# A hybrid decoder layer in one kernel: another queue for token loads, and another order of hand-over for token tiles, partial results, weight sums and counts

## The chip, the core and the metric

The kernel runs on one core of a Trainium2 chip. A core has four compute engines that each take their instructions in order: TensorE for matrix products (with a queue of its own for loading weights into the array), VectorE, ScalarE, and GpSimd. A fifth, SyncE, here only issues DMA transfers; GpSimd and ScalarE issue some too. All transfers are carried out by 16 DMA engines. The metric is the device time of one execution in microseconds (us), the median of several runs.

## What is computed

The reference is one decoder layer with two groups of heads side by side, for 1024 prompt tokens and 8 single decode tokens (1032 tokens in all, each 2048 wide), in float32:

```python
def project(h, w_in, b_i, b_f):          # h = rmsnorm(x): 1032 tokens x 2048
    (aq, ak, av, iq, ik, iw, az, mq, mk, mv, mi, mf, mo, mz) = jnp.split(h @ w_in, split_points, axis=-1)
...
def dsa_prompt(q, k, v, qi, ki, wi):     # sparse attention: the index picks 256 of the earlier tokens
    scores = indexer_scores(qib, ki, wib)          # relu(qi . ki) weighted by wi, summed over 16 heads
    _, idx = lax.top_k(scores, topk)
    return sparse_attend(qb, gather_rows(k, idx), gather_rows(v, idx), valid)
...
def mlstm_run(q, k, v, ig, lf, C0, n0, m0, chunk):   # a recurrent memory, four heads of 128 x 256
...
def merge(x, att_o, p, h_ml, ml_norm_w, w_out):
    a = att_o * jax.nn.silu(p['az'])
    mo = rmsnorm(h_ml) * jax.nn.sigmoid(p['mo']) * jax.nn.silu(p['mz'])
    return x + jnp.concatenate([a, mo], axis=-1) @ w_out
```

The decode tokens do the same against a paged cache of 4096 past tokens each: their index scores over the past are reduced to the best 256 rows, which are gathered from the cache. The outputs are the normalized results of both groups of tokens, the keys and values, and the memory's states.

## The kernel before

**Precision.** A float32 operand of a matrix product is split in two: `H`, the value rounded to the matrix unit's format, and `L`, what is left. A product is the sum of three: H by H, L by H, H by L. So every weight tile and every token tile is cast by ScalarE (`H`) and subtracted by VectorE (`L`) before TensorE uses it. The rows of the profile show such pairs as `wH`, `wL` (weights) and `xH`, `xL` (tokens).

**Stages of TensorE's main work.** A clock of the plan, the *step*, counts tiles of 128 columns of `w_in`; each step is one tile, in four quarters.

1. *Steps 0 to 20, plain projection* (`proj`, matmuls at L1544, 344 or 388 tokens wide). Steps 1 to 8 make the queries of the index, whose results `evac` takes out of the matrix unit's banks and writes as `iqe` (L379). Steps 9 to 20 make the keys `ki` of the index, and the attention's keys, values and queries.
2. *Steps 21 to 60, the gate stage* (`gate_stage`, matmuls at L1727, 258 tokens wide). Forty tiles are taken as twenty 2 x 2 block problems, and each of these is done by Strassen's scheme with seven products instead of eight: 140 products of 48 matmuls. A product has a *kind* from 1 to 7, which says which sum or block of weights, and which sum or block of tokens, it multiplies. The order is: kinds 4 and 6 in pairs (products 0 to 39), all of kind 1 (40 to 59), all of kind 3 (60 to 79), all of kind 2 (80 to 99), kinds 5 and 7 in pairs (100 to 139). After each half of a product `tick` is called: a tick is 1/7 of a step, a product two ticks, so product n begins at step 21 + 2n/7.
3. The output projection (`quarter` and what follows it, matmuls at L2092), again by Strassen's scheme.

**Token tiles.** Strassen's scheme needs five sums and blocks of the tokens (each 2048/2 deep by 516 wide). `job_prep` makes them in steps of `(k, c)`: 16 steps, each loads a tile `X` (`load`, two transfers, L1402), scales it on VectorE (L1410), makes differences in a tile `O` (L1416 and L1417), and stores `O` (L1419) and part of `X` (L1420) to a scratch array `xsD`. It asks for `X` two steps ahead, from three buffers, and has one buffer for `O`. Loads and stores are both issued by GpSimd.
In the gate stage three *slots* of eight tile pairs hold what the products need; a slot is refilled by `fill(slot, op)`, which puts eight entries on a list. Each tick takes one entry off it: a load from `xsD` on SyncE (L1680), and three ticks later its cast and subtraction (L1674 and L1675). `None` on the list is a tick without a load.

**Partials.** Kinds 4 and 6 leave a sum per block that kind 1 adds to, then kind 3, and so on. Each partial is 258 KB: `put` stores it to `spD`, `get` loads it back into one of four buffers `ev` (L1746), and `combine` adds the new product out of the banks (L1822). In the phases of kinds 1, 3 and 2 `ask` is called for the first partial before the phase, and for that of product i + 1 halfway through product i.

**Weight sums.** Kinds 0 to 3 multiply sums of weight blocks. `job_usum` makes these in main memory with DMAs alone: `copy` writes one block to `usD` (L1432), `plus` adds another onto it with an accumulating DMA on GpSimd (L1436). The order is sums 0 and 1 together for all twenty problems, then sum 3 for all, then sum 2 for all. Copies of sums 0 and 3 go out on SyncE, the rest on GpSimd.

**The work beside.** The rest are *jobs*: generators whose `yield` hands back a number of units. Each `Job` has a first step, a last step and a weight (its units in all). Three *lanes* run one job each at a time; at each quarter or tick a lane goes on with its job until the units done are in line with the time left to its last step. A larger `yield` is thus a longer pause before the job's next instructions are put on the list. Lane 0: `gates`, `index` (`job_index`: scores of the prompt's index at L468 to L473, and the choice of its 256 tokens, whose masks `biasS` SyncE stores at L562), `att`, `ml`. Lane 1: `prep`, `dscore`, `dsel` (`job_dsel`: for the decode tokens, a search of the 256th best score bit by bit; each round counts on VectorE into `cb`, L1062, and sums the counts over partitions with a small matmul, L1064), `qrows`, `datt` (gathers at L1294), `dml`. Lane 2: `usum`. `wget`, which gives a product its weights, first runs lane 2 on if the sum isn't made yet.

**What sets the order.** The Python code lists the instructions; a scheduler then plays the list against the engines and fixes each engine's order, work under `tc.high_priority()` first. `pin` (`tc.keep_in_program_order`) holds an instruction behind the one listed just before it on the same engine. On the chip each engine and each queue then goes strictly in that order, waiting on semaphores.

## Time and profile before

| | |
|---|---|
| median of 3 runs | 1986.03 us (1983.48 to 1994.43) |
| the profiled execution | 1999.2 us |
| its span, first to last instruction | 1997.4 us |
| mean granted clock of TensorE | 0.983 |
| TensorE busy | 1910.9 us, 96% of the span, 13422 matmuls |
| VectorE, ScalarE, GpSimd busy | 1406.6, 918.6, 388.6 us |
| moved by DMA | 474.46 MB, 238 GB/s over the span |

How to read it: the span is one profiled execution; busy times leave out instructions that only issue transfers, so SyncE has none. "L1727" is a line of the kernel. In a group of instructions, what is written stands left of the arrow and what is read right of it, then the shapes, then the count, the busy time, the mean of one in ns, and the engine's idle time ahead of them with what ended most of it. "PEld" is TensorE's loading of weights; "SPq" and "POOL" with a DMA are the issuing of transfers by SyncE and GpSimd. "A <- B: x, n, m" in a view of waits says that A waited x us for B in n waits, the longest m us. The granted clock is 1 when TensorE runs at full rate; after an idle time it is lower for a while.

### The profile page before, as it was taken

The page shows a single profiled execution, that of the slowest core. Times are in us where ns is not written, and L with a number is a line of the kernel's source. Part 1 is how long each engine was busy: PE and PEld are TensorE (multiplying, and loading weights), DVE is VectorE, ACT ScalarE, POOL GpSimd, SP SyncE. Part 2 cuts the span into 40 slices and gives each one's busy share as a digit, 9 for nine tenths or more (in the row PEclk, how much of TensorE's full clock was granted, in tenths as well). Part 3 has the DMA queues.
Part 4 walks back from the last instruction along what each step waited for, and adds up shares of the span by engine and source line. Part 5 has one row for each costly group of instructions (what it writes and reads, how often), then busy time and mean ns, then how long its engine had stood idle before and what let it go on. Part 6 is the DMA issues. An engine that isn't in the chain of part 4 may idle for free. (4 is left out here: it accounts for less than half of the span.)

```text
span 1997.4 us, 37376 instructions
## 1 busy us (share of the span) xinstructions
PE 1910.9 (96%) x13422; PEld 1829.6 (92%) x13422; DVE 1406.6 (70%) x3341; ACT 918.6 (46%) x1826; POOL 388.6 (19%) x486
## 2 busy tenths in 40 slices
PE   9979999999979999889999999999999999999997
PEld 9979899999959999778999989999999999977876
DVE  8555658758798797483565656576888676777797
ACT  8112364464255652111455555445556334455645
POOL 0232112231110000232001111001112131107632
PEclk9989999999989999998999999999999999999999
DMA  7577666579865447996888999578998858898866
GB/s 258 168 206 221 192 203 186 167 205 245 271 167 168 157 159 235 353 344 213 255 217 224 291 297 241 153 246 258 293 318 306 226 190 273 276 323 291 286 198 220
DMA packets 252918, 474.46 MB, mean 238 GB/s; under 512 B 40549, under 2 KB 116133, under 8 KB 246333
## 3 DMA queue, kind: packets, MB, share of 16 engines
q1 hardware_dynamic: 217261, 356.70, 54.7%
q0 software_dynamic: 21504, 107.32, 20.6%
q10 hardware_dynamic: 13968, 8.06, 1.4%
q8 instruction: 105, 1.72, 0.4%
q14 instruction: 80, 0.66, 0.1%
HBM read 381.54 MB, written 174.32 MB: 278 GB/s over the span
## 5 line engine op out<-in xcount | busy, mean ns | idle before, releaser
L1727 PE MATMUL pj<-xH 128*128 128x258 f32 x1920 | 550.1, 288 | 21.5 <-DVE ev L1822 20.8
L1727 PE MATMUL pj<-xH,xL 128*128 128x258 f32 x1920 | 550.1, 287 | 1.7 <-issue 1.7
L1727 PE MATMUL pj<-xL,xH 128*128 128x258 f32 x1920 | 548.8, 286 | 0.8 <-issue 0.7
L1727 PEld LDWEIGHTS pj<-xH 128*128 128x128 f32 x1920 | 366.9, 191 | 26.2 <-DVE ev L1822 20.3
L1727 PEld LDWEIGHTS pj<-xH,xL 128*128 128x128 f32 x1920 | 367.7, 192 | 3.5 <-issue 2.5
L1727 PEld LDWEIGHTS pj<-xL,xH 128*128 128x128 f32 x1920 | 367.6, 191 | 2.1 <-issue 0.6
L1544 PE MATMUL pj<-xH,wH 128*128 128x344 f32 (+1 forms) x816 | 267.0, 330 | 12.2 <-DVE iqe L379 11.4
L1544 PE MATMUL pj<-xL,wH 128*128 128x344 f32 (+1 forms) x816 | 266.3, 327 | 0.0
L1544 PE MATMUL pj<-xH,wL 128*128 128x344 f32 (+1 forms) x816 | 266.3, 327 | 0.0
L1436 POOL DMA_DIRECT2D usD<-in_wa_dram x80 | 66.3, 927 | 615.8 <-DMA usD<-in_wa_dram 392.6
L256 ACT CAST wH<-wraw 128x512 fp32r<-128x512 f32 (+2 forms) x151 | 89.7, 608 | 177.8 <-PE pj L1544 83.6
L1544 PEld LDWEIGHTS pj<-xH,wH 128*128 128x128 f32 x816 | 154.7, 190 | 14.4 <-DVE iqe L379 12.3
L1544 PEld LDWEIGHTS pj<-xL,wH 128*128 128x128 f32 x816 | 154.8, 190 | 0.8 <-DVE xL L314 0.3
L1544 PEld LDWEIGHTS pj<-xH,wL 128*128 128x128 f32 x816 | 154.9, 190 | 0.2
L257 DVE TENSOR_TENSOR wL<-wraw,wH 128x512 fp32r<-128x512 f32 (+2 forms) x151 | 103.7, 700 | 54.9 <-ACT wH L256 53.1
L2092 PE MATMUL pj<-wH,sH 128*128 128x512 f32 x336 | 132.0, 393 | 1.2 <-ACT wH L2076 0.9
L2092 PE MATMUL pj<-wL,sH 128*128 128x512 f32 x336 | 126.3, 394 | 6.8 <-DVE wL L2081 6.8
L2092 PE MATMUL pj<-wH,sL 128*128 128x512 f32 x336 | 131.4, 392 | 0.0
L470 ACT ACTIVATE rl<-bank 128x512 f32<-128x512 f32 (+2 forms) x160 | 79.8, 522 | 77.9 <-DVE s L473 30.6
L473 DVE SCALAR_TENSOR_TENSOR s<-rl,wiN,s 128x512 f32<-128x512 f32 (+2 forms) x150 | 94.9, 655 | 21.5 <-ACT rl L470 19.3
L468 PE MATMUL bank<-ki,qi 128*128 128x512 f32 (+2 forms) x320 | 82.3, 378 | 10.0 <-ACT rl L470 4.1
L1710 ACT CAST xH<-wL 128x1024 fp32r<-128x1024 f32 x46 | 48.2, 1049 | 94.5 <-PE pj L1727 37.6
(485 smaller groups left out, 4415.3 us busy)
## 6 DMA issues: line engine op xcount, KB each, us to landing
usD<-in_wa_dram POOLq DMA_DIRECT2D x80, 512.0 KB
wraw<-in_wt_dram SPq DMA_DIRECT2D x144, 256.0 KB
usD<-in_wa_dram SPq DMA_DIRECT2D x40, 512.0 KB
usD<-usD POOLq DMA_DIRECT2D x40, 512.0 KB
wraw<-in_wa_dram SPq DMA_DIRECT2D x78, 256.0 KB
wraw<-in_wo_dram SPq DMA_DIRECT2D x64, 256.0 KB
ev<-spD SPq DMA_DIRECT2D x62, 258.0 KB
spD<-ev SPq DMA_DIRECT2D x60, 258.0 KB
```

The costliest lines, as they stand in the source:

```text
L256: a = SC.copy(H[:, s, :cols], raw[:, s, :cols])
L257: return a, V.tensor_tensor(L[:, s, :cols], raw[:, s, :cols], H[:, s, :cols].bitcast(F32), OP.subtract)
L468: PE.matmul(p[:, :cn], qi[:, h % 4, :], ki[x][:, c0:c0 + cn], start=(x == 0), stop=(x == 1))
L470: SC.activation(r[:, :cn], p[:, :cn], AF.Relu)
L473: v = V.scalar_tensor_tensor(s[:, c0:c0 + cn], r[:, :cn], wv, s[:, c0:c0 + cn], OP.mult, OP.add)
L1436: pin(G.dma_start(usD[n, i], src, accum_op=OP.add, max_dma_last_dim=8192))
L1544: m = PE.matmul(ps[:cols, :cn], w_[:, k, :cols], x_[kk][:, c0:c0 + cn], start=(kk == ends[0] and z == 0), stop=(kk == ends[1] and z == 2))
L1710: SC.copy(H, raw[2])
L1727: PE.matmul(ps[c], w_[:, q, ks], x[y][:, c * CS:c * CS + CS], start=(first and q == 0 and k == 0 and z == 0), stop=(q == 1 and k == 3 and ...
L2092: PE.matmul(ps[b], S_[x][:, b * 128:b * 128 + 128], T_[y], start=(k == 0 and z == 0), stop=(k == 7 and z == 2))
```

## The change

Five things are changed; the computation isn't.

1. `load` of `job_prep` issues the tokens' loads on SyncE instead of GpSimd (32 transfers). The job's last step goes from 11 to 12.
2. `fill` gets a parameter `gap`: after each load that many empty ticks stand on the list (1 by default, 3 for slot 0 ahead of kind 1, 2 for slot 0 ahead of kind 2). The refill of slot 2 for kind 2 moves from ahead of kind 1 to ahead of kind 3.
3. In the phases of kinds 1, 3 and 2 two partials are asked for ahead of the phase, and product i asks for that of product i + 2.
4. `job_usum` becomes two jobs in lane 2: `early sums` (sums 0 and 1, and sum 3 of the first eight problems; steps 9.6 to 28.5) and `late sums` (the rest; steps 33 to 47). Before, one job ran from step 12 to 46.
5. In `job_dsel` the count and its sum over partitions are two functions, `count` and `total`, with a `yield` between them in each round; its weight is 4000 units larger and its last step is 27.5 instead of 26 (`qrows` follows, 28 instead of 27). `index` gets a second `yield 3000` ahead of its first scores, begins at 9.4 instead of 9.6, and ends at step 25 instead of 26.5.

The core of the diff:

```diff
@@ job_index
             for n in range(3):
                 load_q(n)
             yield 3000
+            yield 3000
@@ job_dsel
-            def total(src, n=1):
+            def count(src, n=1):
                 with nc.allow_low_precision("counts"):
                     V.tensor_reduce(cb[:, :n * NB], src, AX.X, OP.add)
+
+            def total(n=1):
                 p = bank()
                 PE.matmul(p[:, :n * NB], onesb, cb[:, :n * NB], start=True, stop=True)
                 return p[:, :n * NB]
...
-                c = total(g3[:, :n].rearrange("p y b g -> p (y b) g"), n).rearrange("p (y b) -> p y b", y=n)
-                yield 1700 if n == 1 else 3400
+                count(g3[:, :n].rearrange("p y b g -> p (y b) g"), n)
+                yield 1200 if n == 1 else 2200
+                c = total(n).rearrange("p (y b) -> p y b", y=n)
+                yield 500 if n == 1 else 1200
@@ job_prep
-                    pin(G.dma_start(X[:, y], A["xT"][k + 8 * y].rearrange("p (h t) -> p h t", h=2)[:, :, c:c + CS]))
+                    pin(SY.dma_start(X[:, y], A["xT"][k + 8 * y].rearrange("p (h t) -> p h t", h=2)[:, :, c:c + CS]))
@@ job_usum
-        for i in range(NP + 1):
+        for i in range((NP + 1) * early):
...
-        for n, src in ((3, None), (2, 1)):
+        for n in (3, 2):
             for i in range(NP):
+                if early != (n == 3 and i < NE):
+                    continue
@@ lanes
-                   Job("index", T_AK + 0.6, 26.5, 3000 + sum(map(ix_weight, groups)), lambda: job_index(groups)),
+                   Job("index", T_AK + 0.4, 25.0, 6000 + sum(map(ix_weight, groups)), lambda: job_index(groups)),
...
-             Lane([Job("usum", T_AK + 3.0, 46.0, 8 * NP, job_usum)])]
+             Lane([Job("early sums", T_AK + 0.6, 28.5, 4 * NP + 2 * NE, lambda: job_usum(True)),
+                   Job("late sums", 33, 47.0, 4 * NP - 2 * NE, lambda: job_usum(False))])]
@@ gate_stage
-        def fill(slot, op):
+        def fill(slot, op, gap=1):
             for k in range(8):
                 fills.append((*slots[slot][k], xsD[op, k]))
+                fills.extend([None] * gap)
...
-        fill(0, 2)
-        fill(2, 1)
+        fill(0, 2, 3)
...
         ask(0, 0)
+        ask(0, 1)
         for i in range(NP):
             ps = two()
-            product(1, i, 1, ps, True, asker(0, i + 1))
+            product(1, i, 1, ps, True, asker(0, i + 2))
             with tc.high_priority():
                 put(1, i, combine(ps, got.pop(0), OP.add))
+        fill(2, 1)
         fill(1, 3)
```

The phases of kinds 3 and 2 get the same two lines for their partials, and the refill of slot 0 ahead of kind 2 a gap of 2.

More of the change, by code (lines that the diff above doesn't have):

```diff
@@ L1067, in job_dsel @@
             V.tensor_scalar(ge, sD, 0.0, None, OP.is_ge)
-            c = total(ge)
+            count(ge)
+            yield 2000
+            c = total()
             V.tensor_scalar(pos, c, float(TOPK), None, OP.is_ge)
@@ L1092, in job_dsel @@
             V.tensor_tensor(eq, sD, bc(tf), OP.is_equal)
-            c = total(ge)
+            count(ge)
+            yield 2000
+            c = total()
             V.tensor_scalar(rr, c, -1.0, float(TOPK), OP.mult, OP.add)
@@ L1423, in body, with job_usum @@
     sums = set()
-    def job_usum():
+    NE = 8
+    def job_usum(early):
         def parts(i):
@@ L1484, in body @@
     lanes = [Lane([Job("gates", 5, T_AK - 0.5, 12500, job_gates),
-                   Job("index", T_AK + 0.6, 26.5, 3000 + sum(map(ix_weight, groups)), lambda: job_index(groups)),
+                   Job("index", T_AK + 0.4, 25.0, 6000 + sum(map(ix_weight, groups)), lambda: job_index(groups)),
                    Job("att", T_G + 8, 44.5, 2 * 2 * sum(2 * (1 + (i + 1) * 0.5) for i in range(8)) + 18, job_att, att_free),
                    Job("ml", T_G + 20, 57.0, 39, job_ml, lo_done)]),
-             Lane([Job("prep", 3, T_AK + 2, 1 + 16 * 2, job_prep),
+             Lane([Job("prep", 3, T_AK + 3, 1 + 16 * 2, job_prep),
                    Job("dscore", T_AK + 3, 18.0, 24 + 128 + 2, job_dscore),
-                   Job("dsel", T_AK, 26.0, 2000 + 31 * 1700 + 10000 + 16 * 2800 + 2000, job_dsel),
-                   Job("qrows", T_G + 0.2, 27, 1, job_qrows),
+                   Job("dsel", T_AK, 27.5, 4000 + 31 * 1700 + 12000 + 16 * 2800 + 2000, job_dsel),
+                   Job("qrows", T_G + 0.2, 28, 1, job_qrows),
                    Job("datt", T_G + 7.5, 32.5, 10000 + 8 * 5000 + 34000 + 5 * 2500 + 8000 + 8000 + 5000, job_datt, ix_free),
                    Job("dml", T_G + 20, 55.0, 28000 + 16 * 2500 + 5000, job_dml, hi_done)]),
-             Lane([Job("usum", T_AK + 3.0, 46.0, 8 * NP, job_usum)])]
+             Lane([Job("early sums", T_AK + 0.6, 28.5, 4 * NP + 2 * NE, lambda: job_usum(True)),
+                   Job("late sums", 33, 47.0, 4 * NP - 2 * NE, lambda: job_usum(False))])]
     gateV = gateS.rearrange("(k p) r -> k p r", p=128)
@@ L1866, in gate_stage @@
         ask(0, 0)
+        ask(0, 1)
         for i in range(NP):
             ps = two()
-            product(1, i, 1, ps, True, asker(0, i + 1))
+            product(1, i, 1, ps, True, asker(0, i + 2))
             with tc.high_priority():
                 put(1, i, combine(ps, got.pop(0), OP.add))
+        fill(2, 1)
         fill(1, 3)
         ask(1, 0)
+        ask(1, 1)
         for i in range(NP):
             ps = two()
-            product(3, i, 0, ps, True, asker(1, i + 1))
+            product(3, i, 0, ps, True, asker(1, i + 2))
             with tc.high_priority():
@@ L1886, in flush @@
                 ready.extend((state["u"], k) for k in ks)
-        fill(0, 0)
+        fill(0, 0, 2)
         ask(2, 0)
+        ask(2, 1)
         for i in range(NP):
             ps = two()
-            product(2, i, 2, ps, True, asker(2, i + 1))
+            product(2, i, 2, ps, True, asker(2, i + 2))
             with tc.high_priority():
```

## The prediction

> **What bounds the kernel now.** I read the page's head first, then the time by stretches, then TensorE's waits, and only after that each engine and queue that ends one of those waits. The page:
>
> ```profile
> span 1997.4 us, 37376 instructions
> PE 1910.9 (96%) x13422; PEld 1829.6 (92%) x13422; DVE 1406.6 (70%) x3341; ACT 918.6 (46%) x1826; POOL 388.6 (19%) x486
> ```
>
> TensorE is the bound, so a change can only win back TensorE's idle time and the half clock that follows it. The stretches (length, then PE, PEld, DVE, ACT, POOL busy with instruction counts, granted clock, DMA share, GB/s) say where those lie:
>
> ```profile
> 75.00:100.00 25.00, 25.00 (x146) 24.95 (x145) 13.94 (x27) 4.45 (x8) 4.46 (x6) 1.00 0.85 256
> 100.00:150.00 50.00, 39.39 (x202) 38.73 (x201) 27.51 (x57) 9.57 (x17) 17.69 (x24) 0.90 0.71 207
> 200.00:225.00 25.00, 21.37 (x123) 20.86 (x122) 9.73 (x21) 5.68 (x12) 4.20 (x6) 0.93 0.95 254
> 225.00:525.00 300.00, 300.00 (x1977) 296.22 (x1976) 213.78 (x616) 146.98 (x320) 63.49 (x71) 1.00 0.69 196
> 550.00:600.00 50.00, 38.07 (x188) 30.19 (x189) 47.90 (x112) 28.55 (x52) 5.26 (x8) 0.90 0.61 162
> 600.00:775.00 175.00, 175.00 (x1450) 173.18 (x1449) 149.88 (x412) 95.55 (x151) 2.11 (x3) 1.00 0.54 166
> 800.00:950.00 150.00, 126.47 (x942) 119.41 (x941) 80.55 (x126) 25.03 (x34) 45.42 (x45) 0.92 0.92 302
> ```
>
> Four losses follow. In 100 to 150 TensorE issues 202 matmuls where the stretch before gives 146 in 25 us, so 292 in 50: 90 are missing, 90/146 x 25 = **15.4 us**. In 200 to 225, 3.6 us are idle and the clock is 0.07 short over 25 us, 1.8: **5.4 us**. In 550 to 600, 11.9 idle and 50 x 0.10 of clock: **16.9 us**. In 800 to 950, at the 1450/175 = 8.29 matmuls per us of 600 to 775, 1243 were due and 942 came: 301/8.29 = **36.3 us** (idle 23.5 and clock 150 x 0.08 = 12 give about the same). Who ends the waits (total, times, longest):
>
> ```profile
> PE pj L1727 <- DVE ev L1822: 20.8, 9, 5.0
> PE pj L1544 <- DVE iqe L379: 11.4, 3, 6.1
> PE bank L1064 <- DVE cb L1062: 6.5, 2, 4.8
> PE bank L468 <- DMA ki<-kS: 3.6, 2, 2.1
> ```
>
> One wait for each loss: evictions of index tiles (first), `ki` (second), the count for dsel (third), the adding of partials (fourth).
>
> **Token loads to SyncE.** VectorE's waits from 75 to 150, GpSimd's and SyncE's from 60 to 260, then GpSimd's queue:
>
> ```profile
> DVE X L1410 <- DMA X<-in_xT_dram: 15.4, 9, 2.3
> DVE O L1416 <- DMA xsD<-O: 14.7, 7, 5.2
> ```
> ```profile
> POOL X L1402 <- DMA xsD<-X: 76.4, 13, 7.3
> ```
> ```profile
> SPq L253 <- DVE wL L257: 35.1, 11, 8.6
> ```
> ```profile
> 109.36 1.45 POOL L1402 DMA_DIRECT2D X<-in_xT_dram  x2 [6.29 <-DMA xsD<-X]
> 110.81 0.77 POOL L1419 DMA_DIRECT2D xsD<-O  x1
> 111.58 0.73 POOL L1420 DMA_DIRECT2D xsD<-X  x1
> 119.61 1.45 POOL L1402 DMA_DIRECT2D X<-in_xT_dram  x2 [7.30 <-DMA xsD<-X]
> ```
>
> A step of prep is a ring: the load of X waits until the store of an earlier X has landed (6.3 us), takes 1.45 us to issue, and the two stores of the step stand behind it on GpSimd. That is one step in 119.6 - 109.4 = 10.2 us. VectorE, bound in order, waits for X and for O, and the eviction of the index tile stands behind those waits. With the loads on SyncE the stores no longer stand behind a waiting load, so O's store leaves earlier; the 15.4 us of waits for X should mostly go, the 14.7 for O partly. Prep also gets 9 steps of the plan instead of 8. All 32 loads now cost SyncE issue time, some 0.4 us each by its rows for tiles of this size further down (1.27 for three), 13 us over the 180 of prep, which its waits cover; behind each one that waits stand weight loads and index stores. The gain lies between 15.4 and, if SyncE's weights come late, a loss (a rival below). O's half is not clearly cured, so I take half, **7.7 us**.
> A rule of the Trainium skill ("DMA: Bandwidth & Descriptors", section "Issuing engines are not separate DMA queues") speaks against this: transfers issued from any engine run on the same 16 DMA engines, so another issuer saves only issue time. By it this term would be near nothing; the row that bears on it is the store standing behind the 6.29 us wait, which is order on a queue and not bandwidth.
>
> **Index, early sums and the ki wait.** The second `yield 3000` lets the plan put 6000 of 25,956 units per step, 0.231 steps, between loading `ki` and the first score, before it was 3000 of 23,782, 0.126. With some 27 us per step (12 tiles from about 201 to 526) that is 2.9 us more lead against 3.6 us of waiting. But sums now start at step 9.6 instead of 12 and prep runs to 12, at a DMA share of 0.95 already. I take **1 us**, between 0 and 5.4. The faster index (9% more units per step) adds at most 0.09 x 213.78 = 19 us of VectorE to 225 to 525, where it is busy 71% and TensorE never stops: nothing.
>
> **dsel's counts.** The whole kernel's row of this matmul:
>
> ```profile
> L1064 PE MATMUL bank<-cb,onesb 128*128 128x24 bf16 (+1 forms) x18 | 3.4, 186 | 6.7 <-DVE cb L1062 6.5
> ```
>
> The same instructions are issued; only the matmul is handed over 1200 or 2200 units (about 0.1 to 0.18 steps) after the count, so products stand before it. Its 6.5 us with their share of the clock, 5.0 x 6.5/11.9 = 2.7, make 9.2 us. But VectorE is busy 47.90 of 50 us there: a count that is late for that reason is late after a step too. Half of it, **5 us**; the ends are 0 and 16.9 (if index and dsel, planned apart now, empty the whole stretch).
>
> **Partials, token tiles, sums.** The product stage from 815 on. First VectorE's waits of 800 to 935 and two of its rows, then SyncE's queue and the count of product matmuls up to 815:
>
> ```profile
> DVE ev L1822 <- DMA ev<-spD: 11.3, 4, 4.8
> ```
> ```profile
> 838.03 0.76 DVE L1822 TENSOR_TENSOR ev<-pj,ev 128x258 f32<-128x258 f32 x2 [1.23 <-DMA ev<-spD]
> ```
> ```profile
> 897.87 0.76 DVE L1822 TENSOR_TENSOR ev<-pj,ev 128x258 f32<-128x258 f32 x2 [4.75 <-DMA ev<-spD]
> ```
> ```profile
> 521.14 1.27 SPq L1680 DMA_DIRECT2D xL<-xsD  x3
> ```
> ```profile
> 823.15 8.94 SPq L1680 DMA_DIRECT2D xL<-xsD  x8
> 832.41 0.32 SPq L1746 DMA_DIRECT2D ev<-spD  x1
> ```
> ```profile
> 526.00:815.00 289.00, 239.68 (x1920) 235.67 (x1920) 0.98 0.65 196
> ```
>
> 1920/48 = 40 products end at 815, so product 41's partial was asked at 832.4, behind a run of eight token tiles that held SyncE 8.9 us, and used at 838.0; TensorE stood 5.0 us. Asking two ahead puts that request in front of the phase and every later one a product, at least 48/8.29 = 5.8 us, earlier, against VectorE waits of at most 4.8. The ring has four buffers: asked two ahead, a buffer is taken again two products after its store was issued, 8 us or more, still longer than a store of this size took above (6.3 to 7.3). So the 11.3 us go, with their share of the clock, 12 x 11.3/23.5 = 5.8: **17.1 us**. The lower end is 0 (requests still late because the transfers are), the upper the whole 36.3.
> The spreading itself I cost at nothing, because in SyncE's rows it already doesn't hold: the first token tiles of the product stage go out at 521, before its first product, though the list puts twenty empty ticks ahead of them. They leave when their buffer is free, and the casts are what the gap moves. If that cover fails the gain is inside the 36.3.
> The sums: GpSimd and SyncE around the end of index.
>
> ```profile
> 643.84 0.52 POOL L1432 DMA_DIRECT2D usD<-usD  x1 [4.75 <-DMA usD<-in_wa_dram]
> 782.35 1.56 POOL L1436 DMA_DIRECT2D usD<-in_wa_dram  x2 [137.99 <-DMA usD<-in_wa_dram]
> ```
> ```profile
> 809.06 1.81 POOL L1294 DMA_INDIRECT ck<-in_ck_dram,idxs  x1 [0.31 <-PE bank L1727]
> ```
> ```profile
> 774.02 0.53 SPq L562 DMA_DIRECT2D biasS<-gt  x1
> 774.60 0.49 SPq L1432 DMA_DIRECT2D usD<-in_wa_dram  x1
> ```
>
> GpSimd stood 138 us for a copy that SyncE issued behind index's last store, then made up its sums in front of the gathers, so that both fell into 800 to 950. With the sums' first part planned to be over at 28.5 and index at 25.0, the copies should be out before that store, and the gathers start free. I count this as the cover for the partials' term and add nothing. The late sums end at step 47, the last is needed by the product at 49.3 (21 + 99 x 2/7), the first of them is made at 38.7 and needed at 43.9: no new wait.
>
> **Sum.** 7.7 + 1 + 5 + 17.1 = 30.8 us. The profiled execution took 1999.2 us, its span and 1.8 around it, so 1968.4; it lies 13 us above the median shown, and I carry the difference over: 1986.0 - 30.8 = **1955 us**.
>
> **Rivals.**
> *The queue doesn't matter* (also the skill's rule above): prep's ring is the landing of its stores, whoever issues the loads. For it: the 14.7 us for O; against it: the 15.4 for X. Without 7.7: 1963.
> *The partials come late anyway*, since transfers and not requests are slow: for it, share 0.92 and 302 GB/s over 150 us; against it, the run of eight in front of the request. Without 17.1: 1972.
> *Product 60 waits for its last token tile.* Its casts are now handed to ScalarE on ticks 83 to 111 instead of 83 to 90, each behind what att was given by then (2.69 units a tick, so 82 units, eight pairs, instead of 26). ScalarE, then product matmuls:
>
> ```profile
> 990.01 1.15 ACT L1674 CAST xH<-xL 128x516 fp32r<-128x516 f32 x2
> ```
> ```profile
> 1059.33 0.62 ACT L617 CAST qH<-qL 128x512 fp32r<-128x512 f32 x1 [0.51 <-PE bank L634]
> ```
> ```profile
> 983.00:1059.00 76.00, 44.36 (x310) 40.08 (x310) 1.00 0.67 188
> ```
>
> The last of these tiles was cast at 990, att's ninth pair was near 1059. If att starts no earlier than now, the 310 product matmuls between move back, 310/8.29 = 37 us. Against it: with gathers earlier, att starts earlier, and from some 70 us before product 60 on it costs nothing. 37 - 30.8: 1992.
> *SyncE becomes the queue that waits* (the slower side). The 76.4 us that GpSimd waits for landed stores move to SyncE between 75 and 255; its slack there is the 35.1 us for which weight loads wait for their buffer. The rest, 41.3, delays weights. It decides where a load of X is issued more than the weights' lead before its store lands, above all after step 9.6, where prep's stores now stand behind sums on GpSimd. 41.3 instead of a gain of 7.7, the others kept: 1986 + 41.3 - 23.1 = 2004. Against it: a store is issued about 10 us, a step, before the load that waits for it and lands in 6 to 7.
>
> **How the numbers follow.** Forecast 0.45 (by itself 1940 to 1972), queue 0.13, partials 0.17, product 60 0.13, SyncE 0.12. About 0.5%, 10 us, is what a measurement can tell from no change: faster is below 1976, slower above 1996. Faster: 0.45 + 0.13 + two thirds of 0.17 = 0.69. Slower: SyncE 0.12 and a quarter of product 60, 0.16 rounded up for mishaps; the rest 0.15. The range goes from 1935 (7.7 more from the first stretch and 12 from the other bounds) to 2003, just under the SyncE case.
>
> **What would show it.** Right: no idle of GpSimd for `xsD<-X`, over 240 matmuls in 100 to 150; no VectorE wait for `ev<-spD` after product 40, and over 1050 matmuls in the 150 us around it; GpSimd without a 138 us wait; `L1064` idle under 4 us. Wrong: SyncE waiting for `xsD<-X` with TensorE waiting for weights before 260; TensorE waiting on `xH L1674` near product 60; token tiles that do leave tick by tick, which would make my nothing for the spreading false.

## The result

The changed kernel takes 2010.95 us (median of 4, 2007.50 to 2013.76), the kernel before 1984.76 us on the same chip: 1.0123 of before, 95% interval 1.0083 to 1.0163, so about 24 us slower. The forecast was 1955 us, the range 1935 to 2003.

Single executions of one kernel scatter by several us: in one comparison 25 of before lay between 1979 and 2003 us. So the ratios below, with their 95% intervals, rest on 4 to 12 executions of a kernel beside before on the same chip. They are estimates over all of these executions and lie up to 0.0024 from the ratio of the two plain medians. One profile shows where time goes only where a stretch moves by much more than two profiles of the same kernel differ. For before there are two, of 1999.2 and 1988.9 us; between 800 and 950 us they lose 35.5 and 29.0 us, and two profiles of another kernel below (`dscore` a step later) lose 30.2 and 39.0 us there.

The head of the page of the changed kernel:

```profile
span 2010.9 us, 37394 instructions
PE 1914.4 (95%) x13422; PEld 1832.6 (91%) x13422; DVE 1412.4 (70%) x3341; ACT 918.1 (46%) x1826; POOL 364.1 (18%) x454
```

TensorE does the same 13422 matmuls; it stands more. Its stretches after the change (length, then PE, PEld, DVE, ACT, POOL busy with counts, granted clock, DMA share, GB/s):

```profile
100.00:150.00 50.00, 47.16 (x247) 45.93 (x246) 33.17 (x68) 10.78 (x19) 8.95 (x12) 0.93 0.85 247
150.00:200.00 50.00, 46.32 (x263) 44.84 (x263) 23.09 (x54) 9.51 (x17) 8.41 (x11) 0.97 0.70 212
250.00:350.00 100.00, 89.81 (x562) 88.71 (x561) 60.36 (x222) 45.87 (x116) 20.58 (x24) 0.95 0.75 200
550.00:650.00 100.00, 84.84 (x591) 80.72 (x590) 80.81 (x223) 55.80 (x91) 10.49 (x15) 0.91 0.84 241
800.00:950.00 150.00, 136.36 (x1086) 131.27 (x1085) 90.97 (x162) 28.01 (x38) 37.80 (x37) 0.94 0.84 268
950.00:1150.00 200.00, 184.56 (x1401) 175.54 (x1400) 125.14 (x342) 107.75 (x263) 18.66 (x27) 0.98 0.85 234
```

The same of before where the prediction did not show it, first profile, and below it the second profile of before from 800 on:

```profile
150.00:200.00 50.00, 49.22 (x287) 48.06 (x286) 28.10 (x60) 11.02 (x20) 13.51 (x19) 1.00 0.74 222
250.00:350.00 100.00, 100.00 (x662) 99.79 (x661) 69.30 (x235) 51.30 (x128) 21.29 (x22) 1.00 0.66 193
550.00:650.00 100.00, 88.07 (x591) 79.27 (x592) 92.01 (x243) 57.95 (x98) 7.37 (x11) 0.95 0.60 167
950.00:1150.00 200.00, 195.79 (x1567) 191.71 (x1566) 122.16 (x319) 102.74 (x237) 20.91 (x31) 1.00 0.86 249
```
```profile
800.00:950.00 150.00, 131.49 (x982) 123.45 (x982) 81.38 (x130) 25.65 (x35) 49.47 (x48) 0.93 0.95 313
950.00:1150.00 200.00, 198.23 (x1587) 194.35 (x1586) 127.57 (x331) 108.49 (x250) 20.19 (x30) 1.00 0.86 250
```

Loss is here, as in the prediction, idle time plus length times the clock that is missing (where the clock is low while TensorE stands it counts that twice, so it is a measure to compare by, not a sum). It changed like this (before has two values where its two profiles are shown):

| stretch | before | changed | forecast of the change |
|---|---|---|---|
| 100 to 150 | 10.6 + 5.0 = 15.6 | 2.8 + 3.5 = 6.3 | -7.7 |
| 150 to 200 | 0.8 | 3.7 + 1.5 = 5.2 | 0 |
| 200 to 225 | 3.6 + 1.8 = 5.4 | 3.0 + 1.8 = 4.7 | -1 |
| 250 to 350 | 0 | 10.2 + 5.0 = 15.2 | 0 |
| 550 to 650 | 11.9 + 5.0 = 16.9 | 15.2 + 9.0 = 24.2 | -5 |
| 800 to 950 | 35.5 and 29.0 | 13.6 + 9.0 = 22.6 | -17.1 |
| 950 to 1150 | 4.2 and 1.8 | 15.4 + 4.0 = 19.4 | 0 |

The gains of 100 to 150 and of 800 to 950 are there, the first for another reason, the second smaller and not far beyond what two profiles of one kernel differ by. But two stretches where TensorE hardly stood lose 15 us, and 15 to 18 us, more than before, and 550 to 650 another 7. TensorE's two longest waits in each:

```profile
PE bank L1029 <- DVE bd L1024: 7.3, 1, 7.3
PE pj L1557 <- DVE im L531: 2.5, 1, 2.5
```
```profile
PE bank L688 <- ACT ptH L683: 5.8, 10, 0.9
PE bank L635 <- ACT xH L582: 5.6, 1, 5.6
```

In the first stretch the two waits are for `dscore`'s operand `bd` and for a step of index (`im`), both made by VectorE. VectorE is late with both because it stands 10.0 us for a weight tile of the projection, whose transfer ScalarE waits for:

```profile
313.07 0.62 ACT L256 CAST wH<-wraw 128x512 fp32r<-128x512 f32 x1 [9.94 <-DMA wraw<-in_wa_dram]
```

The second stretch has two parts. Between 975 and 1050 TensorE is busy 68.96 of 75 us at full clock; it waits for attention's own chain (`ptH` is its weights after the softmax), which it meets bare when it has no product to do beside it. Between 1050 and 1100 it is busy 41.65 of 50 us at a clock of 0.93, and there ScalarE waits for the transfer of a tile of attention's keys:

```profile
1088.82 1.05 ACT L582 CAST xH<-xL 128x1024 fp32r<-128x1024 f32 x1 [8.03 <-DMA xL<-akS]
```

### The profile page after: what moved, and what is told of

It reads as the page before. It is cut to its first block, busy times and chain, and to the rows that moved or that the text cites. A ratio compares the mean times of both kernels' runs of the same rounds, so it can differ in the third digit from the quotient of the medians.

```text
span 2010.9 us, 37394 instructions
## 1 busy us (share of the span) xinstructions
PE 1914.4 (95%) x13422; PEld 1832.6 (91%) x13422; DVE 1412.4 (70%) x3341; ACT 918.1 (46%) x1826; POOL 364.1 (18%) x454
## 4 chain that ended last, share of the span: by engine, by line
PE 70%; DMA 14%; DVE 9%; issue 3%; ACT 3%; SPq 1%; POOL 1%; ACTq 0%; POOLq 0%; DVEq 0%
PE pj L1741 29%; PE pj L1557 13%; PE bank L1741 5%; PE bank L2042 5%; PE pj L2109 4%; PE bank L688 2%; PE bank L635 2%; PE bank L469 2%; PE bank L1557 2%; DMA wraw<-in_wa_dram 2%; PE bank L1029 1%; PE bank L679 1%; DMA wraw<-in_wt_dram 1%; DVE wL L2098 1%; DMA xL<-xsD 1%
## 5 line engine op out<-in xcount | busy, mean ns | idle before, releaser
L1741 PE MATMUL pj<-xH 128*128 128x258 f32 x1920 | 547.4, 287 | 14.7 <-DVE ev L1836 14.0
L1557 PE MATMUL pj<-xH,wH 128*128 128x344 f32 (+1 forms) x816 | 268.5, 332 | 10.2 <-DVE iqe L379 6.4
L1724 ACT CAST xH<-wH 128x1024 fp32r<-128x1024 f32 x46 | 48.2, 1047 | 100.7 <-PE pj L1741 53.0
```

The lines of the kernel that those rows point to most:

```text
L1557: m = PE.matmul(ps[:cols, :cn], w_[:, k, :cols], x_[kk][:, c0:c0 + cn], start=(kk == ends[0] and z == 0), stop=(kk == ends[1] and z == 2))
L1724: SC.copy(H, raw[2])
L1741: PE.matmul(ps[c], w_[:, q, ks], x[y][:, c * CS:c * CS + CS], start=(first and q == 0 and k == 0 and z == 0), stop=(q == 1 and k == 3 and ...
```

## The experiments

**Is it the spreading of token tiles?** ScalarE's casts of slot 0's last seven tiles in the changed kernel, and the first product matmuls of kind 3 (about 48, a product's worth); then the same stretch before:

```profile
979.05 0.63 ACT L1688 CAST xH<-xL 128x516 fp32r<-128x516 f32 x1
989.07 0.63 ACT L1688 CAST xH<-xL 128x516 fp32r<-128x516 f32 x1
998.17 0.63 ACT L1688 CAST xH<-xL 128x516 fp32r<-128x516 f32 x1
1013.39 0.63 ACT L1688 CAST xH<-xL 128x516 fp32r<-128x516 f32 x1
1019.74 0.62 ACT L1688 CAST xH<-xL 128x516 fp32r<-128x516 f32 x1
1029.61 0.64 ACT L1688 CAST xH<-xL 128x516 fp32r<-128x516 f32 x1
1040.56 0.64 ACT L1688 CAST xH<-xL 128x516 fp32r<-128x516 f32 x1
975.70:1022.20 46.50, 8.07 (x51) 6.57 (x49) 1.00 0.66 175
```
```profile
976.70:991.40 14.70, 7.01 (x50) 6.15 (x48) 1.00 0.93 328
```

One cast comes every 6 to 15 us, each behind what ScalarE does for attention, and the matmuls of product 60, which needs all eight tiles, and of 61 come as the tiles do: a product's worth takes 46.5 us instead of 14.7. The change without part 2:

```diff
-        fill(0, 2, 3)
+        fill(0, 2)
+        fill(2, 1)
...  (gap 0 in the others; fill(2, 1) no longer ahead of kind 3)
```

> The change without the spreading of token tiles (fill as before: no empty ticks, and slots 0 and 2 refilled ahead of kind 1). Theory 'casts behind attention': in the changed kernel the casts of slot 0 for kind 3 go out one by one, at 979, 989, 998, 1013, 1020, 1030, 1041, each behind the attention work that ScalarE was given before it, so product 60 takes 46 us and TensorE, left with attention alone, loses 23 us between 950 and 1150 against 6 before. Without the spreading 17 us come back: 1991 to 1997, product 60 under 20 us. Rival 'any order': the loss belongs to the order of the whole list and not to these tiles; then the time stays above 2003 and the loss between 950 and 1150 above 15 us.

Measured: 1.0026 (1.0001 to 1.0052), 0.97% or 19 us below the whole change. Its row:

```profile
950.00:1150.00 200.00, 196.57 (x1564) 190.52 (x1563) 123.98 (x322) 102.19 (x235) 13.50 (x19) 1.00 0.79 226
```

The loss there is 3.4 us, as before the change. And part 2 alone:

> Before, with the spreading of token tiles alone. Theory 'casts behind attention': 17 us more than before, 2000 to 2005, and product 60 above 35 us. Rival 'any order': the tiles alone do not do it, since attention starts no earlier than before; within 8 us of before, product 60 under 20 us.

Measured: 1.0056 (1.0031 to 1.0081), 11 us slower; the first 48 product matmuls of kind 3 take 36.1 us, the loss of 950 to 1150 is 8.5 + 2.0 = 10.5 us:

```profile
950.00:1150.00 200.00, 191.53 (x1472) 183.80 (x1472) 128.78 (x351) 111.89 (x269) 24.25 (x35) 0.99 0.89 253
```

So the spreading is harmful in both surroundings, by 19 and 11 us (whether it is more so in the whole change the intervals leave open), and the "any order" rival falls. That the late casts hold up products 60 and 61 is shown. That they make the whole 19 us isn't: 6.0 us of idle time stand beside them (975 to 1050), most of the rest at the key tile. The weight sums alone, with no spreading, also lose 8.0 + 6.0 = 14.0 us between 950 and 1150. The change without part 5 keeps the spreading, begins product 60 later, at 1009 us, and does it in 13.8 us, yet loses 11.0 + 6.0 = 17.0 us. And part 2 also moves the refill of slot 2, which wasn't tried apart from the gaps.

The kernel before, run again for its second profile:

> The kernel before, unchanged, for a second profile. The profiled execution of before lies 13 us above its median (1999.2 against 1986.0), that of the change does not, so the comparison of the two profiles shows 13 us of losses against 26 us between the medians. Theory 'one place': the new profile is at 1982 to 1990 and the 13 us are missing in one stretch, most likely 800 to 950 us, where the first profile loses 37 us of TensorE time with the DMA engines busy 0.92. Rival 'everywhere': the difference is spread over all stretches in pieces below 3 us. Time against before: ratio 1.000, interval holding 1.

Ratio 0.998 (0.9951 to 1.0009). The second profile is 10 us shorter. Between 800 and 950 it loses 6.5 us less, and the rest is spread in small pieces, so neither theory holds fully. It set the measure for what a profile can tell.

**Is it the plan of index and dsel?** The change without part 5:

> The change with index and dsel planned and written as before (no second pause ahead of the scores, count and its sum in one step, last steps 26.5 and 26). Theory 'plan': the 14 us that TensorE newly loses between 250 and 350 (VectorE's bd 7.4 us late, VectorE standing 10 us for a weight tile ahead of it) and the 12.9 us between 600 and 650 (two counts of dsel, 5.8 and 6.3 us) come from the new order of index and dsel: without it the first are gone, and the second are back between 550 and 600, 1993 to 1999 in all. Rival 'sums and token loads': the loss of 250 to 350 comes from the weight sums that now start at step 9.6, or from prep; it stays, and the time is 2005 to 2015.

Measured: 1.0119 (1.0071 to 1.0168), the same as with it. Its loss of 250 to 350 is 10.2 + 7.0 = 17.2 us:

```profile
250.00:350.00 100.00, 89.85 (x556) 88.42 (x556) 59.57 (x220) 45.70 (x114) 25.22 (x29) 0.93 0.76 210
```

So part 5 makes neither a gain in time nor that loss; the first half of the theory named for it falls. The second half holds in its place: without part 5 the loss of 600 to 650 is back between 550 and 600 (9.8 + 6.0 = 15.8 us, and 0.6 us after it), and the time doesn't change. What it did to the counts the whole kernel's row of that matmul shows (before: 6.7 us idle, 6.5 of them for `cb`):

```profile
L1067 PE MATMUL bank<-cb,onesb 128*128 128x24 bf16 (+1 forms) x18 | 3.4, 186 | 11.8 <-DVE cb L1063 11.8
```

In the changed kernel these are two waits, of 5.6 us at 601 and 6.2 us at 616. Ahead of the first VectorE is busy 10.63 of the 11 us from 590 to 601. Ahead of the second it stands for the store of a partial, whose buffer it needs again:

```profile
615.27 0.43 DVE L1836 TENSOR_TENSOR ev<-pj,rstd 128x258 f32<-128x258 f32 x1 [6.35 <-DMA spD<-ev]
```

**The other parts one by one.** The token loads on SyncE with prep's later end (part 1), the two jobs of sums (part 4), the asking (part 3):

> Before, with the token loads on SyncE and prep's last step at 12, nothing else. Theory 'prep pays it back': 8 us less TensorE loss between 100 and 150, of which 2 to 5 come back between 150 and 250, and 14 us of new loss between 250 and 350, because dscore, next in prep's lane, now starts straight after prep and its first data is late: 5 to 11 us slower than before (1.003 to 1.006). Rival 'sums': the loss of 250 to 350 is made by the weight sums that start at 9.6, so it is absent here: 3 to 8 us faster (0.996 to 0.998).

> Before, with the weight sums in two jobs, nothing else. Theory 'prep pays it back': no loss between 250 and 350, and within 5 us of before. Rival 'sums': 10 to 15 us lost there by copies that go out on SyncE from step 9.6 on, between the transfers of prep and dscore; 1.005 or more. The prediction costed this part at nothing.

> Before, with partials asked two products ahead, nothing else. The prediction: 17.1 us faster (0.991). Theory 'eight in flight': in SyncE's rows of the changed kernel an issue that waits for a transfer waits for the landing of the one issued eight before (831.40 landed at 846.39, and the ninth issue is at 846.45; the same at 849.6, 852.2 and 853.4), so a run of eight token tiles in a stretch of slow landings stops SyncE for 10 to 15 us however early the list has the request; the gain is 5 to 10 us (0.995 to 0.9975) and one product of the 41st to 44th still takes over 15 us.

Measured: 1.0067 (1.0042 to 1.0093), 1.0057 (1.0032 to 1.0082), 1.0028 (0.9996 to 1.0061). With the spreading's 1.0056 none of the four gains anything alone; they add up to 2.1%, more than the 1.2% of all together. The rows of 250 to 350 for the sums and of 800 to 950 for the asking, then VectorE's longest wait of 800 to 950 in before and with the asking:

```profile
250.00:350.00 100.00, 93.55 (x598) 92.39 (x597) 62.62 (x223) 46.15 (x115) 23.71 (x26) 0.98 0.80 219
```
```profile
800.00:950.00 150.00, 129.04 (x958) 121.96 (x958) 81.38 (x128) 25.19 (x35) 44.54 (x46) 0.92 0.95 308
```
```profile
DVE xL L1711 <- ACT xH L1710: 29.9, 8, 11.9
```
```profile
DVE xL L1711 <- ACT xH L1710: 22.5, 11, 6.4
```

Both the loads and the sums make a loss between 250 and 350 where there was none, 10.0 and 8.5 us, so "sums" and "prep pays it back" were both half right. The asking leaves 33.0 us of loss between 800 and 950, as before, although VectorE's waits for partials there fall to 5.2 us, from 11.3 and 9.1 us in the two profiles of before. VectorE waits longer there for ScalarE's casts of weight tiles (L1710; these tiles share buffers with others, so the row has other names), and the asking leaves most of that.

**The queue or the later end?** Part 1 is two edits. Each alone, on before:

```diff
-  pin(G.dma_start(X[:, y], ...))                  # token loads on SyncE, prep's last step still 11
+  pin(SY.dma_start(X[:, y], ...))
...
-  Job("prep", 3, T_AK + 2, ...)                   # the other kernel: last step 12, loads on GpSimd
+  Job("prep", 3, T_AK + 3, ...)
```

> Before, with the token loads on SyncE, prep's last step left at 11. The kernel with the loads on SyncE and the last step at 12 was 1.0067 of before: 7 us less loss between 100 and 150, 5 us more between 150 and 200, and 10 us of new loss between 300 and 350, where dscore's first gathers are late. Theory 'dscore's start': the last two belong to the later end of prep, which takes away the free step between prep and dscore; without it no loss between 250 and 350, and 3 to 8 us faster than before (0.996 to 0.9985). Rival 'queue': SyncE's order makes them; 1.004 to 1.007 as before.

> Before, with prep's last step at 12 instead of 11 and the token loads left on GpSimd. Theory 'dscore's start': the loss of about 10 us between 300 and 350 is here too, 1.003 to 1.007. Rival 'queue': no such loss, and within 3 us of before, or a little faster since prep has more time between 100 and 150.

Measured: 1.0006 (0.9984 to 1.0028) for the queue, 1.0044 (1.0016 to 1.0071) for the end. The queue alone, from 100 on, and TensorE's longest wait between 100 and 250; then the later end alone, and TensorE's longest wait between 250 and 350:

```profile
100.00:150.00 50.00, 42.63 (x229) 40.49 (x228) 30.05 (x62) 9.39 (x17) 8.96 (x12) 0.97 0.81 229
150.00:200.00 50.00, 45.43 (x237) 43.59 (x237) 28.84 (x63) 9.76 (x18) 7.95 (x11) 0.89 0.80 222
```
```profile
PE pj L1544 <- DVE wL L257: 10.4, 2, 5.9
```
```profile
100.00:150.00 50.00, 46.39 (x247) 45.55 (x246) 29.58 (x61) 11.60 (x20) 15.16 (x21) 0.93 0.80 238
250.00:350.00 100.00, 93.28 (x602) 92.83 (x601) 62.93 (x218) 47.31 (x121) 21.75 (x25) 0.97 0.66 197
```
```profile
PE bank L1028 <- DMA kp<-in_cik_dram,idx: 5.9, 1, 5.9
```

This settles where the smaller loss of part 1 comes from. What made 100 to 200 faster is the later end: with the loads still on GpSimd it loses 3.6 + 3.5 = 7.1 us, all of it before 150, and VectorE's waits for X from 75 to 150 fall from 15.4 to 0.5 us. The queue alone lowers the loss of 100 to 150 too, to 7.4 + 1.5 = 8.9 us, but loses 4.6 + 5.5 = 10.1 us right after it: 19.0 us in all, against 16.4 and 19.3 us in the two profiles of before. VectorE still waits 13.4 us for X, and TensorE now waits 10.4 us for weights that SyncE brings late instead of for evicted index tiles. In the kernels with the later end the loss at 300 is the end's: `dscore` follows prep in its lane, and its first gather is late. (By "DMA: Bandwidth & Descriptors" of the Trainium skill, section "Issuing engines are not separate DMA queues", another issuer saves issue time alone; the ratio of 1.0006 agrees.)

Giving `dscore` its step back (`T_AK + 4` on top of the later end):

> Before, with prep's last step at 12 (token loads left on GpSimd) and dscore's first step at 13 instead of 12. With the last step alone the loss between 100 and 200 fell from 16.3 to 7.2 us and 9 us of new loss stood between 300 and 350, where TensorE waits 6.1 us for dscore's first gather. Theory 'dscore's start': the free step between the two jobs is what the gather needs; the new loss goes, the gain stays, 5 to 9 us faster than before (0.9955 to 0.9975). Rival 'any order': the new loss stays or moves elsewhere; 0.999 to 1.005.

> The same kernel as the one with prep's last step at 12 and dscore's first step at 13 (0.9982 of before, 0.9958 to 1.0005), timed longer. Theory 'the gain is real': 6 us of loss fewer between 100 and 350 than before in its profile; 0.996 to 0.9985 with an interval below 1. Rival: it was scatter; the interval holds 1.

Measured: 0.9982 (0.9958 to 1.0005) and 0.9986 (0.9966 to 1.0006). Of the loss between 250 and 350, 3.4 + 2.0 = 5.4 and 6.0 + 2.0 = 8.0 us stay; TensorE waits there for index's work on VectorE (`im`, L545, 3.4 and 3.6 us) instead of for the gather, and VectorE stands behind a weight tile there too (7.4 and 6.4 us). Both times 0.14 to 0.18% faster with an interval that just holds 1: a gain isn't shown.

The change without part 2 and with `dscore` a step later:

> The change without the spreading of token tiles and with dscore's first step at 13. The change without the spreading was 1.0026 of before and lost 13 us between 250 and 350. Theory 'dscore's start': these go: 0.995 to 0.998. Rival 'sums': the weight sums that start early make that loss as well (alone they lost 8 us there), so 8 to 10 of them stay: 1.000 to 1.003.

Measured: 1.0054 (1.0034 to 1.0074), no better than without that step; the loss of 250 to 350 is 6.0 + 2.0 = 8.0 us, about what the sums alone make. Both kernels show the late weight tile of the whole change: ScalarE's longest wait for one in this stretch is 8.3 us here and 10.6 us with the sums alone, and before has none. The later end alone has one of 6.7 us, and the change without the early sums wasn't tried, so how the two share that loss stays open. Why the rest got slower its one profile (1985.2 us, the fastest of its executions) can't tell.

**Why does asking earlier not help?** SyncE's issues in the changed kernel from product 40 on, what SyncE waited for longest between 838 and 856, and what VectorE waited for:

```profile
831.40 9.84 SPq L1694 DMA_DIRECT2D xL<-xsD  x8
846.45 0.32 SPq L1771 DMA_DIRECT2D gateS<-ev  x1
...
852.21 0.32 SPq L1760 DMA_DIRECT2D ev<-spD  x1
```
```profile
SPq L1771 <- DMA xL<-xsD: 5.1, 1, 5.1
```
```profile
854.40 0.35 DVE L1340 TENSOR_SCALAR bias<-bias,cc 64x256 f32<-64x256 f32 x1 [12.09 <-DMA bias<-in_cst_dram]
859.74 0.76 DVE L1836 TENSOR_TENSOR ev<-pj,ev 128x258 f32<-128x258 f32 x2 [1.76 <-DMA ev<-spD]
```

The eight token tiles of slot 2, which the list now has ahead of kind 3, some 140 us later, still go out here in one run. After them SyncE's next issue waits 5.1 us for a token tile: the first of the run, issued at 831.40, lands at 846.39, and the issue comes at 846.45. It is the eighth before. Of the 242 instructions of SyncE whose wait ended with the landing of one of SyncE's own transfers, 142 waited for exactly the eighth before, 182 of 273 in the kernel before. So a run of slow transfers stops SyncE, and what stands behind it is late however early it was listed. Here that is not only the partial, asked at 852.21, but first a small tile of the decode attention (`bias`), issued at 848.15, for which VectorE stands 12.09 us. Product 43 takes 19.3 us.

Five kernels are meant to take one side away. Loads held in the list's order, with one empty tick per tile, on top of the asking; this keeps the spreading from failing on SyncE:

```diff
-                    SY.dma_start(l.bitcast(F32), src)
+                    pin(SY.dma_start(l.bitcast(F32), src))
```

> Before, with partials asked two ahead, slot 2's tiles moved ahead of kind 3, one empty tick after each token tile, and each token tile's load held on SyncE behind the instruction listed ahead of it, so that it can't leave as soon as its buffer is free. Theory 'eight in flight': no run of eight tiles on SyncE near 831; products 40 to 50 take under 8 us each, the loss between 800 and 950 falls below 20 us, and the time is 8 to 15 us below the kernel with the asking alone (0.985 to 0.992 of before). Rival 'the transfers are slow': the DMA engines are busy 0.9 there whatever is issued first; the loss stays above 28 us and the time within 4 us of the kernel with the asking alone.

Measured: 0.9996 (0.9971 to 1.0021). Products 42 to 46 take 5.7 us each, then product 47 takes 16.3:

```profile
850.00:875.00 25.00, 17.07 (x137) 16.87 (x136) 20.14 (x23) 2.73 (x3) 13.60 (x13) 0.87 1.01 336
```

The stall has moved from 836 in the kernel with the asking alone to 863, with the DMA engines full (a share of 1.01, 336 GB/s); the loss of 800 to 950 is 17.2 + 9.0 = 26.2 us, between the two theories.

The sums' copies on GpSimd, so that GpSimd doesn't stand 138 us:

> Before, with all copies of the weight sums issued on GpSimd instead of half of them on SyncE. In before GpSimd waits 138 us, from 644 to 782, for a copy that SyncE issues behind index's last store, and makes up its sums between 800 and 900, where the DMA engines are busy 1.0 and transfers take 15 us. Theory 'transfers are slow': without that wait no sums are made up there, the DMA share between 800 and 900 falls below 0.85, and the loss between 800 and 950 falls from 37 and 32 us (two profiles of before) below 18: 10 to 20 us faster (0.990 to 0.995). Rival 'requests are late': what is asked late stays late; loss above 28 us and within 5 us of before; and GpSimd, which then also waits for its own copies, may delay dscore's gathers between 260 and 460.

Measured: 1.0138 (1.0091 to 1.0185), 27 us slower, which neither theory had. The loss of 800 to 950 is 22.4 + 10.5 = 32.9 us with the DMA engines as full (share 0.95, 310 GB/s). But the sums aren't made ahead: GpSimd now stands still from 603 to 798, for what a gather ahead of them needs, and issues 25 transfers of the sums between 800 and 950, where GpSimd and SyncE together issue 24 in before:

```profile
798.26 1.06 POOL L1294 DMA_INDIRECT ck<-in_ck_dram,idxs  x1 [194.91 <-DVE pb L1274]
```

So this kernel doesn't tell the theories apart.

Without the accumulating transfers (the weights are then not summed), without and with the early asking, and without sixteen token tiles:

> Before without the accumulating transfers of the weight sums (80 transfers of 512 KB left out; products then use weights that aren't summed). It measures what the traffic of the sums costs at most. Theory 'transfers are slow': the loss between 800 and 950 falls below 12 us, between 200 and 225 (the wait for ki) it goes as well, and the kernel is 25 to 40 us faster (0.980 to 0.9875). Rival 'requests are late': 5 to 12 us faster, with the loss between 800 and 950 above 25.

> Before with partials asked two ahead and without the accumulating transfers of the weight sums (80 transfers of 512 KB left out, the weights aren't summed). Without these transfers alone the kernel took 0.9958 of before, with the loss between 800 and 950 at 26 us, and with the asking alone 1.0028, at 32. Theory 'traffic': asking early pays once the transfers are fast: below 0.990, and the loss between 800 and 950 under 12 us. Rival 'a run ahead on SyncE': the token tiles still stop SyncE, which takes an issue only when the one eight before has landed; 0.994 to 0.999, loss above 20.

> Before with partials asked two ahead and without the loads of the sixteen token tiles for kinds 1 and 2 that go out between 800 and 835 (4 MB left out of 35 MB that move between 800 and 900; the products use the old tiles). Theory 'a run ahead on SyncE': no run of eight, no request behind it; the loss between 800 and 950 under 12 us, 0.988 to 0.992 of before. Rival 'traffic': the DMA engines stay busy 1.0 between 800 and 900 and a partial takes 12 us or more; loss above 20 us, 0.996 to 1.001.

Measured: 0.9958 (0.9938 to 0.9978), 0.9937 (0.9913 to 0.9961), 1.0036 (1.0016 to 1.0055). The losses of 800 to 950 are 33.8, 26.3 and 25.6 us: none under 12. The first two don't thin out the traffic of that stretch either. Without the accumulations GpSimd's copies of the sums fall into it (with 11 more by SyncE), and 326 and 336 GB/s move there, against 302 and 313 in the two profiles of before. GpSimd's copies from 800 to 950 in the first:

```profile
usD<-usD POOLq DMA_DIRECT2D x20, 512.0 KB, 13.4
```

In the last kernel the run is gone and 800 to 850 hardly loses, but then comes this (stretch, then the issue of a partial on SyncE and VectorE's row that waited for it):

```profile
850.00:875.00 25.00, 18.64 (x135) 18.02 (x134) 20.11 (x23) 3.71 (x6) 14.48 (x13) 0.86 1.03 351
```
```profile
864.17 0.35 SPq L1747 DMA_DIRECT2D ev<-spD  x1
```
```profile
884.18 0.76 DVE L1823 TENSOR_TENSOR ev<-pj,ev 128x258 f32<-128x258 f32 x2 [4.88 <-DMA ev<-spD]
```

A partial of 258 KB takes 20 us from issue to landing. Two products ahead are 11.6 us. So the request is early and the transfer slow: without the run of token tiles, slow transfers alone still stop a product, and the time is no better than with the asking alone (1.0036 and 1.0028). No kernel here took both away. The sums really leave the stretch only with part 4 (alone: 11 transfers of sums, share 0.85, 275 GB/s), and that kernel loses 25.9 us there. How much each holds stays open.

**A version that beats both.** The later end of prep, `dscore` a step later, asking two ahead, slot 2's tiles ahead of kind 3, one empty tick per tile, and loads of tiles held in the list's order:

> The same with partials asked two ahead, slot 2's tiles ahead of kind 3, one empty tick per tile, and token loads held in the list's order on SyncE (these alone: 0.9996 of before, against 1.0028 with the asking alone). Theory 'parts add': 0.995 to 0.998. Rival 'any order': what one part gains another stretch gives back; 0.998 to 1.003.

Measured: 0.9922 (0.9894 to 0.9949), 1978.47 us against 1992.87. The parts' ratios multiply to 0.9986 x 0.9996 = 0.998; it is 0.6% faster than that. Its rows:

```profile
100.00:150.00 50.00, 47.33 (x267) 46.37 (x266) 28.06 (x59) 11.89 (x21) 14.13 (x20) 1.00 0.78 235
800.00:950.00 150.00, 136.22 (x1019) 127.43 (x1018) 92.52 (x157) 33.82 (x51) 42.24 (x41) 0.94 0.95 313
```

It keeps the gain of 100 to 150 (loss 2.7) and loses 22.8 us between 800 and 950, where before loses 35.5 and 29.0. Why the parts give more together than one by one isn't settled by these runs.

## Why the prediction was wrong, step by step

**Token loads, 7.7 us.** The loss of 100 to 150 did fall by 9 us, but the step failed in its cause, so the right size is luck. I took the store behind a waiting load for what made VectorE wait. With the queue alone VectorE still waits 13.4 us for X where it waited 15.4, and the ratio is 1.0006. The smaller loss belongs to the later end of prep, which I had beside it in half a sentence ("9 steps of the plan instead of 8"). And I did not look at what follows prep in its lane: `dscore`'s first gather, 5.9 us late, with the clock 10 us. The rival that SyncE becomes the waiting queue was right in kind: weights are late by 10.4 us in the kernel with the queue alone; its 41.3 us were four times too many. The rival that the queue doesn't matter was right. (The 6.3 and 7.3 us that the prediction takes for a store's time are only GpSimd's waits for its landing, so they are lower bounds.)

**The wait for `ki`, 1 us, and index.** 0.7 us less loss, near the forecast, but not shown: the two profiles of before lose 5.4 and 7.0 us there, so they differ by more. "Nothing" for 225 to 525 failed by 15 us, though not through the index's pace, as the kernel without part 5 shows. A weight tile comes 9.9 us late there; prep's later end and the early sums each make such a loss alone.

**Counts, 5 us.** It failed: the counts are 11.8 us late instead of 6.5. The doubt beside the term, a busy VectorE, holds for the first of the two waits; the second is VectorE's own wait of 6.35 us for a partial's store, which the step didn't consider. The DMA share from 550 to 650 rose from 0.60 to 0.84, and that the early sums slowed the store is likely but not shown.

**Partials, 17.1 us.** The loss of 800 to 950 fell by 6 to 13 us, but the asking alone does nothing measurable (1.0028). The failed step is "So the 11.3 us go, with their share of the clock": it took VectorE's waits for partials for what makes TensorE's loss. With the asking they fall to 5.2 us and the loss stays at 33.0. In the same stretch VectorE waited 29.9 us for casts of weight tiles, a larger row that the step left out; in the changed kernel its longest wait, 12.09 us, is for a tile that SyncE issues late. Nor does 5.8 us cure a transfer that takes 20 us, or a request behind a run that stops SyncE for 10 to 15 us. My sign for the term, over 1050 matmuls in the stretch, came true (1086), but with fewer sums in it (11 transfers instead of 24), so it doesn't speak for the asking. The rival "the partials come late anyway" fits the measured time better: transfers are slow there, at a share of 0.92 to 1.0 of the DMA engines. I gave it 0.17 and priced it as a gain lost.

**The spreading, costed at nothing.** The loads leave when their buffer is free, as I read: slot 2's tiles go out at 831 whatever the list says. But "the casts are what the gap moves" I left to a rival with 0.13, and this is the largest single loss, 19 us in the whole change. Its mechanism was as described there, casts behind attention at product 60. Its price was off: 37 us as if TensorE stood, where attention ran in its place. TensorE loses 6.0 us beside the late casts and about 12 more at attention's key tile after them; that the casts make this second part isn't shown.

**Sums, costed at nothing.** Alone they are 1.0057. They seem to lower the loss of 800 to 950 (TensorE busy 134.63 us at 0.93, so 25.9 us), by little more than two profiles of before differ, but add 8.5 us between 250 and 350 and 9.8 us or more between 950 and 1150. GpSimd's long wait stayed in the changed kernel, 132 us instead of 138:

```profile
POOL usD L1446 <- DMA usD<-in_wa_dram: 382.3, 16, 132.1
```

**The sum and the chances.** I gave the forecast 0.45 and slower 0.16, and let the rivals come one at a time: two took a term away, two added one loss, and none had several terms fail together. Each of the four parts measured alone costs something or gives nothing.

## What to carry to other kernels

- Before an instruction is spread or put later, look at what its engine will have been given by then: a cast handed over a few ticks later stood behind a whole stage of attention, and 48 matmuls, a product's worth, took 46 us. Moving the load is another matter than moving the cast.
- A request made earlier helps only if the transfer was waiting to be asked, and only if the engine that waits for it has no longer wait beside it. Take the time from issue to landing at the busiest point, and see whether the issuing queue itself stands behind its own earlier transfers.
- When a job's window is widened, price the job that follows it in the same lane; and test edits that travel together one at a time, since here the half of a part that lowered a loss (prep's later end) was hidden behind the other half (the queue).
- When a kernel takes something away to test a cause, count whether it is gone from the stretch in question. Three kernels here that were to relieve 800 to 950 of the sums moved 25 and 31 of their transfers through it, where before moves 24.

## What the runs showed of the hardware that was not expected

- SyncE often issues a transfer only when the eighth before it has landed (142 of its 242 waits for transfers of its own in the changed kernel). The trace points to the program rather than the queue: SyncE's 1413 transfers use eight semaphores in turn, and 1186 of them have in them or just ahead of them a wait for the semaphore that they then use.
- A transfer of 258 KB took 20 us with the DMA engines full at 351 GB/s, where one asked at 832.41 in the kernel before had landed by 838.03. In the kernel before, two asked at 871.1 and 879.7 already took 15.0 and 18.1 us.
